# A two-layer transformer with a product-key expert layer: expert panels prepared on another queue, gate columns one batch ahead, another order of the expert blocks

## The chip, the cores and the metric

One core of one Trainium2 chip runs the kernel. The metric is the device time of one execution in microseconds; of several runs the median is shown. TensorE is called PE, VectorE DVE, ScalarE ACT, GpSimd POOL and SyncE SP, as in the profile.

## What is computed

The input is x, 512 tokens of 1024 floats. Block 1 has two layers, each an attention mixer (stick-breaking and sparse attention in the first, forgetting attention in the second) and a feed-forward layer with a convolution and a gate. Block 2 is a neighbourhood attention with a gated MLP, and then the layer that most of the change is about: PEER, a feed-forward layer of 128 x 128 experts, each one row u and one row v. A token's query picks 16 experts in each of 8 heads:

```
idx, g = top-16 of product keys (two tables of 128), softmax over the 16
y[t] = sum over the 128 picked (head, k):  g * gelu(h[t] . u[idx]) * v[idx]
x = rmsnorm(x + gate * y)
```

All of it is float32. The weights of the 16384 experts are read as 128 panels `peer_u[i]` and 128 panels `peer_v[i]`, each 128 x 1024 (512 KB).

## The kernel before, in words

**Matmuls in three parts.** A float32 product is made of three matmuls of a reduced type: high x high, high x low, low x high (`mm3`, L175 to L181). A weight panel is loaded by SP into `raw` (L166), its high part `wh` is cast by ACT (L168) and its low part `wl` is the difference, made by DVE (L173). `raw`, `wh` and `wl` have three buffers each. A scheduler orders the instructions of each engine when the program is built; every engine then runs its list in order. SP's list holds the loads, and an issue that waits holds up all behind it.

**Panels made ahead.** While the feed-forward layer of layer 1 (`ffn(1)`, L866, 1036 to 1290 us of the trace) runs, `pre_steps` (L134) splits the first NPRE = 48 panels of `peer_u` for PEER: a load into one of three quarters of the tile `pre` (L139, L142), the cast on ACT into the fourth quarter (L145), the difference on DVE over the loaded data (L146), and a store of it to the DRAM tensor `Ul` (L148). Loads and stores are SP's. `ffn` takes one step after each panel `wi` and after each token tile. Later `prep_now` loads `wl` from `Ul` for panels below NPRE (L171) in place of the difference L173.

**PEER's stages.** 384 of the 512 tokens go through all panels as dense matmuls, with a gate matrix that is zero for the experts not picked; the last 128 tokens have their rows fetched one by one, by POOL's indirect loads ("gathers", 512 KB each, L1354, into the tiles `ring` and `gat`): 128 of u, used on DVE as dot products with `h2t` (L1362), and 128 of v, added into `acc` on DVE (L1373). A gather starts after a one-column POOL copy (L1353) that waits for a recent tile, so that gathers follow the program; its use comes GD = 6 gathers later.

- Top-k: `peer_topk` picks the experts while `u_block` (L1330) runs u panels beside it: matmuls, a gelu on ACT (L1338), and a store of the activations to `Ad`.
- Gates (2045 to 2296 us): `peer_g` (L1628) builds the gate matrix of 16 tokens at a time, 24 batches. Two tables `oB` and `Ag` of ones and zeros on DVE (L1633, L1636), a product on DVE for 8 tokens (L1639) and 8 scalings on ACT for the others (L1643), 32 matmuls on PE (L1648), four copies on ACT into `gst` (L1649) and a store to `Gd`. Beside each batch one or two u panels run, and two gathers are called for with their uses.
- v stage (2330 us to the end): 128 blocks, one v panel each. SPILL = 72 blocks have their activations in `Ad` and load them as `A` (L1445); the other 56 ("fresh") run their u panel now. A block multiplies the activations by `G` (eight blocks' gates, L1440, three buffers), splits the result into `wth` and `wtl` (L1463, L1465), and runs 18 matmuls over the v panel into six PSUM banks. The first 5 blocks are fresh; then spilled and fresh ones alternate until the fresh ones are used up, and 21 spilled blocks come last. After each block 214/118 gathers are called for. The last LASTV = 3 blocks run bank by bank, with the final norm (`finish`, L1476) behind.

Of the kernel before, what the change touches and what calls it, by code (L numbers as in the profile page):

```python
# [15 lines left out]
AF = mybir.ActivationFunctionType  # L16
ALU = mybir.AluOpType
# [4 lines left out]
P = 128  # L22
# [11 lines left out]
NKEY = 128  # L34
TB = 16
TD = T - P
NTB = TD // TB
GI = 8
GD = 6
SPILL = 72  # L40
NPRE = 48
FIRST = 5
LASTV = 3
EG = 10
GSTOP = 3
# [5 lines left out]
class Builder:  # L51
# [82 lines left out]
    def pre_steps(self):  # L134

        nc = self.nc
        b = self.big.tile([P, 4, D], F32, name="pre", tag="big")
        hi, u = b[:, 3].bitcast(F32R), self.I["peer_u"]
        nc.sync.dma_start(b[:, 0], u[0])  # L139
        for i in range(NPRE + 1):  # L140
            if i + 1 < NPRE:
                nc.sync.dma_start(b[:, (i + 1) % 3], u[i + 1])  # L142
            if i < NPRE:
                r = b[:, i % 3]
                nc.scalar.copy(hi, r)  # L145
                nc.vector.tensor_sub(r.bitcast(F32R), r, hi)  # L146
            if i:
                nc.sync.dma_start(self.Ul[i - 1], b[:, (i - 1) % 3])  # L148
            yield

    def look_ahead(self):
# [714 lines left out]
    def ffn(self, l, filler=None, ctx=None, pre=None):  # L866
        nc, tc, I = self.nc, self.tc, self.I
        h = self.norm_t()
        pre = pre or iter(())
        wi, wo = I[f"ffn_wi{l}"], I[f"ffn_wo{l}"]  # L870
        with ExitStack() as cx:
            ap = cx.enter_context(tc.tile_pool(name="ffp", bufs=1))
            gp = cx.enter_context(tc.tile_pool(name="ffg", bufs=2))
            if ctx:
                next(ctx)
            cv = ap.tile([P, NF, 4], F32, name="cv")
            nc.sync.dma_start(cv, I[f"ffn_cv{l}"])
            for f0 in range(NF % GF - GF, NF, GF):
                fs = list(range(max(f0, 0), f0 + GF))
                gh = gp.tile([P, GF, T], F32R, name="gh")  # L880
                gl = gp.tile([P, GF, T], F32R, name="gl")
                for q, f in enumerate(fs):
                    if f == 0:
                        first = self.panels_h([wi[0], wi[1]], h)
                    pa = first.pop(0) if first else self.panel_a(wi[2 * f], h)
                    next(pre, None)
                    pb = first.pop(0) if first else self.panel_a(wi[2 * f + 1], h)
                    next(pre, None)
                    tm = gp.tile([P, T], F32, name="tm")
                    nc.scalar.activation(tm, pa, AF.Identity, scale=cv[:, f, 2:3], bias=cv[:, f, 3:4])  # L890
                    nc.vector.scalar_tensor_tensor(tm[:, 1:], pa[:, :T - 1], cv[:, f, 1:2], tm[:, 1:],
                                                   op0=ALU.mult, op1=ALU.add)
                    nc.vector.scalar_tensor_tensor(tm[:, 2:], pa[:, :T - 2], cv[:, f, 0:1], tm[:, 2:],
                                                   op0=ALU.mult, op1=ALU.add)
                    silu = nc.scalar.activation(tm, tm, AF.Silu)
                    nc.vector.tensor_mul(tm, tm, pb)
                    nc.scalar.copy(gh[:, q], tm)
                    nc.vector.tensor_sub(gl[:, q], tm, gh[:, q])
                    if filler:
                        filler()  # L900
                    if ctx and f == 3:
                        next(ctx)
                if f0 + GF == NF:
                    self.sqrt_table(silu)
                w = []
                for f in fs:
                    raw = self.wp.tile([P, D], F32, name="raw", tag="raw", bufs=3)
                    nc.sync.dma_start(raw, wo[f])
                    wh = gp.tile([P, D], F32R, name="woh", bufs=5)
                    nc.scalar.copy(wh, raw)  # L910
                    wl = gp.tile([P, D], F32R, name="wol", bufs=5)
                    nc.vector.tensor_sub(wl, raw, wh)
                    w.append((wh, wl))
                for t in range(NT):
                    for c in range(2):
                        ps = self.st_() if c else self.tt_()
                        for q in range(len(fs)):
                            self.mm3(ps, (gh[:, q, t * P:(t + 1) * P], gl[:, q, t * P:(t + 1) * P]),
                                     (w[q][0][:, c * T:(c + 1) * T], w[q][1][:, c * T:(c + 1) * T]),
                                     q == 0, q == len(fs) - 1)  # L920
                        xs = self.x[:, t, c * T:(c + 1) * T]
                        nc.vector.tensor_add(xs, xs, ps)
                    next(pre, None)
                    if f0 + GF == NF and t == 1 and self.nx:
                        self.norm_half()
# [372 lines left out]
    def peer(self):  # L1298
        nc, tc, I = self.nc, self.tc, self.I
        self.look = 0  # L1300
        with ExitStack() as c0:
# [3 lines left out]
            Gd = dp.tile([NTB, P, NKEY, TB], F32, name="Gd")  # L1305
            ap = ec(tc.tile_pool(name="pep", bufs=1))
            wk = ec(tc.tile_pool(name="pew", bufs=2))
# [21 lines left out]
            last = [None]  # L1329
# [61 lines left out]
                    yield  # L1391

            gs = gathers()
            gk = ExitStack()
            ep = gk.enter_context(tc.tile_pool(name="pee", bufs=2))
            with ExitStack() as ck:
                kk = ck.enter_context(tc.tile_pool(name="pek", bufs=2))
                steps = self.peer_topk(kk, h, idx, it128, eid, g3, ep)
                for kind in steps:
                    if kind is None:  # L1400
                        break
                    if kind:
                        u_block()
            gp = gk.enter_context(tc.tile_pool(name="peg", bufs=2))
            for tb in range(NTB):
                behind[0] = self.peer_g(gp, idx, it128, tb, Gd)
                if tb == 4:
                    next(steps, None)
                u_block()
                if tb % 2:  # L1410
                    u_block()
                for _ in range(2 if tb < NTB - GSTOP else 0):
                    next(gs, None)
# [9 lines left out]
            rest = list(range(spilled, NKEY))  # L1423
            back = list(range(spilled))
            order, rest = rest[:FIRST], rest[FIRST:]
            while rest or back:
                if back:
                    order.append(back.pop(0))
                if rest and len(rest) * (len(back) + 1) >= len(back) * 1:
                    order.append(rest.pop(0))  # L1430
            early = {i: u_block(True, n < 4) for n, i in enumerate(order[:FIRST])}
            st = {}
            ng = 2 * P - 2 * (NTB - GSTOP)
            NM = NKEY - EG

            def g_load(n):
                k = order[n] // GI
# [59 lines left out]
            for n, i in enumerate(order[:NKEY - LASTV]):  # L1497
                w = nxt
                nxt = v_pre(n + 1)
                v = self.prep(I["peer_v"][i])  # L1500
                for t in range(NT - 1):
                    for c in range(2):
                        v_mm(n, t, c, w, v)
                for _ in range(min(ng, ng * (n + 1) // NM) - min(ng, ng * n // NM)):
                    next(gs, None)
            for _ in gs:
                pass
# [117 lines left out]
        yield None  # L1625
        flush()

    def peer_g(self, wk, idx, it, tb, Gd):  # L1628

        nc = self.nc  # L1630
        ia, ib, g = idx
        oB = wk.tile([P, TB, NKEY], F32, name="oB")
        nc.vector.tensor_tensor(oB, it.unsqueeze(1).broadcast_to([P, TB, NKEY]),  # L1633
                                ib[:, tb * TB:(tb + 1) * TB].unsqueeze(2).broadcast_to([P, TB, NKEY]), op=ALU.is_equal)
        Ag = wk.tile([P, TB, NKEY], F32, name="Ag")
        last = nc.vector.tensor_tensor(Ag, it.unsqueeze(1).broadcast_to([P, TB, NKEY]),  # L1636
                                       ia[:, tb * TB:(tb + 1) * TB].unsqueeze(2).broadcast_to([P, TB, NKEY]), op=ALU.is_equal)
        n = TB // 2
        last = nc.vector.tensor_tensor(Ag[:, 0:n], Ag[:, 0:n],  # L1639
                                       g[:, tb * TB:tb * TB + n].unsqueeze(2).broadcast_to([P, n, NKEY]), op=ALU.mult)  # L1640
        for t in range(n, TB):
            tt = tb * TB + t
            nc.scalar.activation(Ag[:, t], Ag[:, t], AF.Copy, scale=g[:, tt:tt + 1])  # L1643
        st = wk.tile([P, NKEY, TB], F32, name="gst")
        for q in range(TB // 4):
            ps = self.tt_() if q % 2 else self.st_()
# [1 line left out]
                nc.tensor.matmul(ps[:, t * P:(t + 1) * P], oB[:, q * 4 + t], Ag[:, q * 4 + t], start=True, stop=True)  # L1648
            nc.scalar.copy(st[:, :, q * 4:q * 4 + 4].rearrange("p i t -> p t i"), ps.rearrange("p (t i) -> p t i", t=4))  # L1649
        nc.sync.dma_start(Gd[tb], st)  # L1650
        return last


    def run(self, stages):
# [179 lines left out]
```

## Time and profile before

| | us |
|---|---|
| median of 3 runs | 3111.69 |
| lowest and highest run | 3098.77, 3112.72 |
| profiled execution, its own time | 3097.51 |
| its span in the trace | 3095.7 |
| PE busy | 3011.1 (97%) |
| feed-forward layer 1 in the trace | 1036 to 1290 |
| PEER's gates | 2045 to 2296 |
| v stage | 2330 to 3096 |

Busy time of one engine says little by itself here, since PE is busy 97% of the span; what is read are the stretches in which it is not, and what it waits for in them. The trace is of one execution, whose time lies 14.2 us under the median of the runs. A wait is written "engine line <- what ended it". A window's row shows, for its stretch, each engine's busy time, the clock that PE was granted (1.00 is the full one) and the share of time in which the DMA engines were moving data.

### The profile page before, as it was taken

Reading aid. Unit: us, or ns where it says so; the run is one execution under the profiler, and the core shown is the slowest. Engines: PE = TensorE matmul, PEld = TensorE weight load, DVE = VectorE, ACT = ScalarE, POOL = GpSimd, SP = SyncE. Lnnn points to the kernel's source line nnn. Section 1 sums busy time; section 2 is a strip of 40 time slices with the busy share of each in tenths; the row PEclk is TensorE's granted clock in tenths of the full one; section 3 lists DMA queues with packets and bytes.
Section 4 is the critical chain, followed back from the end, with each engine's and each line's share of the span. In section 5 each row is a group of like instructions: output and inputs, shape, how many; then the busy total and the mean of one; then the engine's idle time right before and its main releaser. Section 6 shows DMA issues by size and latency. Waiting matters only on the chain. (4 is left out here: it accounts for less than half of the span.)

```text
span 3095.7 us, 42567 instructions
## 1 busy us (share of the span) xinstructions
PE 3011.1 (97%) x15688; PEld 2548.0 (82%) x15688; DVE 2152.5 (70%) x3986; ACT 1419.3 (46%) x2398; POOL 579.4 (19%) x609
## 2 busy tenths in 40 slices
PE   8999999999999999999999999999899999999988
PEld 6877787788777777788888889999898888888876
DVE  3378798645577766546853689848857777787878
ACT  4466532224455554335663344467663333333333
POOL 2400000000000000000000100013335565554552
PEclk9999999999999999999999999999999999999999
DMA  4210266524211689534332326899789899999986
GB/s 133 69 42 22 90 190 221 186 82 138 92 55 50 210 302 310 198 105 138 108 102 89 116 77 209 285 341 330 265 298 322 303 342 320 336 322 339 317 315 217
DMA packets 224073, 617.88 MB, mean 200 GB/s; under 512 B 20684, under 2 KB 89452, under 8 KB 220396
## 3 DMA queue, kind: packets, MB, share of 16 engines
q1 hardware_dynamic: 186424, 479.87, 46.7%
q0 software_dynamic: 36864, 134.23, 12.0%
q8 instruction: 124, 2.03, 0.3%
q10 hardware_dynamic: 576, 1.05, 0.1%
q14 instruction: 85, 0.70, 0.1%
HBM read 547.34 MB, written 67.73 MB: 199 GB/s over the span
## 5 line engine op out<-in xcount | busy, mean ns | idle before, releaser
L168 ACT CAST wh<-raw 128x1024 fp32r<-128x1024 f32 (+1 forms) x478 | 501.0, 1048 | 974.5 <-PE mm L180 348.6
L173 DVE TENSOR_TENSOR wl<-raw,wh 128x1024 fp32r<-128x1024 f32 (+1 forms) x412 | 504.6, 1228 | 388.0 <-ACT wh L168 384.6
L179 PE MATMUL mm<-bh,wh 128*128 128x384 f32 (+2 forms) x1656 | 599.1, 362 | 4.7 <-ACT wh L168 4.5
L181 PE MATMUL mm<-bh,wl 128*128 128x384 f32 (+2 forms) x1656 | 594.9, 359 | 2.4 <-DVE wl L173 1.5
L180 PE MATMUL mm<-bl,wh 128*128 128x384 f32 (+2 forms) x1656 | 595.1, 359 | 0.0
L179 PEld LDWEIGHTS mm<-bh,wh 128*128 128x128 f32 x1656 | 311.7, 188 | 37.6 <-ACT wh L168 6.5
L181 PEld LDWEIGHTS mm<-bh,wl 128*128 128x128 f32 x1656 | 311.6, 188 | 34.5 <-DVE wl L173 3.3
L180 PEld LDWEIGHTS mm<-bl,wh 128*128 128x128 f32 x1656 | 311.8, 188 | 30.7 <-issue 0.3
L180 PE MATMUL acc<-wl,wth 128*128 128x512 f32 x768 | 303.3, 395 | 11.9 <-DVE wl L173 11.7
L181 PE MATMUL acc<-wh,wtl 128*128 128x512 f32 x768 | 302.7, 394 | 0.0
L179 PE MATMUL acc<-wh,wth 128*128 128x512 f32 x768 | 292.4, 391 | 4.1 <-ACT wth L1463 2.3
L179 PE MATMUL mx<-bh,wh 128*128 128x512 f32 (+3 forms) x616 | 228.1, 370 | 0.0
L180 PE MATMUL mx<-bl,wh 128*128 128x512 f32 (+3 forms) x616 | 225.2, 366 | 0.0
L181 PE MATMUL mx<-bh,wl 128*128 128x512 f32 (+3 forms) x616 | 225.0, 365 | 0.0
L1137 POOL MEMSET bt<- 128x256 f32 x2 | 0.6, 316 | 1043.0 <-PE sc L181 1043.0
L180 PEld LDWEIGHTS acc<-wl,wth 128*128 128x128 f32 x768 | 145.6, 190 | 44.4 <-DVE wl L173 15.1
L179 PEld LDWEIGHTS acc<-wh,wth 128*128 128x128 f32 x768 | 145.0, 189 | 34.3 <-ACT wth L1463 3.1
L181 PEld LDWEIGHTS acc<-wh,wtl 128*128 128x128 f32 x768 | 145.7, 190 | 31.1 <-DVE wtl L1465 0.9
L181 PEld LDWEIGHTS mx<-bh,wl 128*128 128x128 f32 (+1 forms) x616 | 115.2, 187 | 16.1 <-DVE wl L173 0.3
L179 PEld LDWEIGHTS mx<-bh,wh 128*128 128x128 f32 (+1 forms) x616 | 115.2, 187 | 15.6 <-issue 0.7
L180 PEld LDWEIGHTS mx<-bl,wh 128*128 128x128 f32 (+1 forms) x616 | 115.3, 187 | 15.1 <-issue 0.5
L1463 ACT CAST wth<-w 128x384 fp32r<-128x384 f32 x128 | 65.6, 513 | 92.2 <-DVE w L1459 81.6
(593 smaller groups left out, 6147.7 us busy)
## 6 DMA issues: line engine op xcount, KB each, us to landing
raw<-in_peer_u SPq DMA_DIRECT2D x128, 512.0 KB, 5.1
raw<-in_peer_v SPq DMA_DIRECT2D x128, 512.0 KB, 6.8
raw<-in_ffn_wi SPq DMA_DIRECT2D x88, 512.0 KB, 4.4
araw<-in_ada_w SPq DMA_DIRECT2D x48, 512.0 KB, 4.1
pre<-in_peer_u SPq DMA_DIRECT2D x48, 512.0 KB, 5.3
Ul<-pre SPq DMA_DIRECT2D x48, 512.0 KB, 5.2
wl<-Ul SPq DMA_DIRECT2D x48, 512.0 KB, 4.7
Gd<-gst SPq DMA_DIRECT2D x24, 1024.0 KB, 7.3
```

Of the source, the lines that this page charges most:

```text
L168: nc.scalar.copy(wh, raw)
L173: (nc.gpsimd if on_pool else nc.vector).tensor_sub(wl, raw, wh)
L179: nc.tensor.matmul(out, ah, bh, start=first, stop=False)
L180: nc.tensor.matmul(out, ah, bl, start=False, stop=False)
L181: nc.tensor.matmul(out, al, bh, start=False, stop=last)
L1137: nc.gpsimd.memset(bt[:, 4], 0.0)
L1463: nc.scalar.copy(wh, w)
```

## The change

1. NPRE goes from 48 to 32, and the loads and stores of `pre_steps` are issued by POOL. `ffn` gets the steps only from its fourth column group on.
2. `peer_pair` makes `oB` and `Ag` for the next batch right after the matmuls of this one. Six gathers are issued in top-k.
3. The v stage's order spreads the 51 fresh blocks evenly among the 72 spilled ones.
4. Gathers are called for in proportion to a weight of 1 for a spilled block and 2 for a fresh one.

```diff
-NPRE = 48
+NPRE = 32
...
-                nc.sync.dma_start(b[:, (i + 1) % 3], u[i + 1])
+                nc.gpsimd.dma_start(b[:, (i + 1) % 3], u[i + 1])
...
-                nc.sync.dma_start(self.Ul[i - 1], b[:, (i - 1) % 3])
+                nc.gpsimd.dma_start(self.Ul[i - 1], b[:, (i - 1) % 3])
...
-        pre = pre or iter(())
+        steps, pre = pre or iter(()), iter(())
...
-                    if ctx and f == 3:
-                        next(ctx)
+                    if f == 3:
+                        if ctx:
+                            next(ctx)
+                        pre = steps
...
+                    if n > 28 and n % 4 == 0:
+                        next(gs)
+                        ng -= 1
...
+            behind[0], pair = self.peer_pair(gp, idx, it128, 0)
             for tb in range(NTB):
-                behind[0] = self.peer_g(gp, idx, it128, tb, Gd)
+                self.peer_g(gp, pair, tb, Gd)
+                if tb + 1 < NTB:
+                    behind[0], pair = self.peer_pair(gp, idx, it128, tb + 1)
...
-            while rest or back:
-                if back:
-                    order.append(back.pop(0))
-                if rest and len(rest) * (len(back) + 1) >= len(back) * 1:
-                    order.append(rest.pop(0))
+            nr, nb = len(rest), len(back)
+            for n in range(nr + nb):
+                order.append((rest if (n + 1) * nr // (nr + nb) > n * nr // (nr + nb) else back).pop(0))
...
-            NM = NKEY - EG
+
+            wt = [1 if i < spilled else 2 for i in order[:NKEY - EG]]
+            due = [ng * sum(wt[:n]) // sum(wt) for n in range(len(wt) + 1)]
...
-                for _ in range(min(ng, ng * (n + 1) // NM) - min(ng, ng * n // NM)):
+                for _ in range(due[n + 1] - due[n] if n < len(wt) else 0):
                     next(gs, None)
```

`peer_pair` holds the DVE and ACT part of the old `peer_g`, unchanged; its lines are now L1643 (both tables) and L1646 (the product). The lists of instructions move so:

**SP in the feed-forward layer 1.** Before, where the steps begin (L139, L142 and L148 are the steps', L166 and L908 the layer's panels):

```order
107 L877 DMA cv<-in_ffn_cv 128x88
108 L139 DMA pre<-in_peer_u 128x1024
109 L142 DMA pre<-in_peer_u 128x1024 x2
110 L148 DMA Ul<-pre 128x1024
111 L166 DMA raw<-in_ffn_wi 128x1024
112 L142 DMA pre<-in_peer_u 128x1024
113 L148 DMA Ul<-pre 128x1024 x2
114 L142 DMA pre<-in_peer_u 128x1024
115 L166 DMA raw<-in_ffn_wi 128x1024
```

Now, the same place on SP:

```order
107 L877 DMA cv<-in_ffn_cv 128x88
108 L166 DMA raw<-in_ffn_wi 128x1024 x2
109 L910 DMA raw<-in_ffn_wo 128x1024 x2
110 L166 DMA raw<-in_ffn_wi 128x1024 x8
```

and on POOL, which had only fills and copies there:

```order
59 L1062 COPY fold<-idn 32x32 x4
60 L139 DMA pre<-in_peer_u 128x1024
61 L142 DMA pre<-in_peer_u 128x1024 x2
62 L148 DMA Ul<-pre 128x1024
63 L142 DMA pre<-in_peer_u 128x1024
64 L148 DMA Ul<-pre 128x1024 x2
```

The steps have left SP's list and stand in POOL's in the same pattern. On ACT the first cast L145 stands at the same place of the list as before. Before, 29 casts stand among the first 23 of the layer's panel casts and 48 among 42; now all 32 stand among the first 23.

**DVE in the gate stage.** Before, at the fourth and fifth batch (L1362 is the use of a gather, row tiles `ring` and `gat`):

```order
2523 L1633 TENSOR_TENSOR oB<-it_15199,ix_15197 128x2048
2524 L1636 TENSOR_TENSOR Ag<-it_15199,ix_15196 128x2048
2525 L1639 TENSOR_TENSOR Ag<-Ag,ix_15198 128x1024
2526 L1362 ISA ring,act_15203<-ring,h2t 128x1024
2527 L1362 ISA act_15203 128x1
2528 L1362 ISA gat,act_15203<-gat,h2t 128x1024
2529 L1362 ISA act_15203 128x1
2530 L1633 TENSOR_TENSOR oB<-it_15199,ix_15197 128x2048
```

Now, from the first batch on:

```order
2503 L1643 TENSOR_TENSOR oB<-it_15135,ix_15133 128x2048
2504 L1643 TENSOR_TENSOR Ag<-it_15135,ix_15132 128x2048
2505 L1643 TENSOR_TENSOR oB<-it_15135,ix_15133 128x2048
2506 L1646 TENSOR_TENSOR Ag<-Ag,ix_15134 128x1024
2507 L1643 TENSOR_TENSOR Ag<-it_15135,ix_15132 128x2048
2508 L1646 TENSOR_TENSOR Ag<-Ag,ix_15134 128x1024
2509 L1364 ISA ring,act_15139<-ring,h2t 128x1024
2510 L1364 ISA act_15139 128x1
2511 L1364 ISA gat,act_15139<-gat,h2t 128x1024
2512 L1364 ISA act_15139 128x1
2513 L173 TENSOR_TENSOR wl<-raw,wh 128x1024 x7
2514 L1643 TENSOR_TENSOR oB<-it_15135,ix_15133 128x2048
```

Uses (now L1364) begin behind the second batch's tables, not behind the fourth's: 42 of them fall among the 24 batches, where 36 did. Some differences `wl` have moved in between.

**SP at the end of the v stage.** Before, the last blocks are spilled ones:

```order
687 L1445 DMA A<-Ad 128x384
688 L166 DMA raw<-in_peer_v 128x1024
689 L1445 DMA A<-Ad 128x384
690 L166 DMA raw<-in_peer_v 128x1024
```

Now they are mixed, and the last block is a fresh one:

```order
519 L1453 DMA A<-Ad 128x384 x2
520 L166 DMA raw<-in_peer_u 128x1024
521 L166 DMA raw<-in_peer_v 128x1024 x3
522 L1453 DMA A<-Ad 128x384
523 L166 DMA raw<-in_peer_u 128x1024
524 L166 DMA raw<-in_peer_v 128x1024 x2
```

The `G` loads, which from the third on stood 7 to 11 v panels ahead of their first use in the list of SP before, stand 0 to 3 ahead of it for five of the sixteen now, since a new one takes the buffer of one that is needed longer.

## Rows read from the trace of the kernel before

**Rows 1.** The page: busy us of each engine, share of span, instructions.

```profile
PE 3011.1 (97%) x15688; PEld 2548.0 (82%) x15688; DVE 2152.5 (70%) x3986; ACT 1419.3 (46%) x2398; POOL 579.4 (19%) x609
```

**Rows 2.** Windows by stage: busy us of each engine, then clock, DMA share and GB/s.

```profile
1036.00:1182.00 146.00, 136.05 (x613) 109.32 (x612) 103.05 (x125) 80.13 (x106) 0.00 (x0) 0.99 0.87 293
1182.00:1290.00 108.00, 103.90 (x449) 83.19 (x448) 69.27 (x76) 47.29 (x55) 0.00 (x0) 1.00 0.84 286
...
2045.00:2296.00 251.00, 235.95 (x1594) 234.48 (x1593) 195.32 (x165) 186.13 (x347) 92.10 (x84) 0.97 0.86 307
...
2330.00:2985.00 655.00, 652.74 (x3143) 574.00 (x3142) 513.48 (x653) 240.31 (x320) 359.80 (x382) 1.00 0.93 325
2985.00:3020.00 35.00, 24.08 (x95) 18.92 (x94) 24.16 (x28) 7.62 (x10) 21.26 (x17) 0.85 0.84 293
3020.00:3096.00 76.00, 64.08 (x270) 50.81 (x268) 63.63 (x91) 26.71 (x47) 21.54 (x21) 0.94 0.60 216
```

**Rows 3.** Waits of PE, 1036 to 1290 us: total us, times, longest us.

```profile
PE mm L179 <- ACT wh L168: 4.5, 3, 3.0
```

**Rows 4.** Waits of SP's queue, 1036 to 1290 us.

```profile
SPq L148 <- DVE pre L146: 72.4, 29, 7.9
SPq L142 <- DMA Ul<-pre: 48.3, 34, 3.7
```

**Rows 5.** The tile `pre`, 1036 to 1290 us: each line's ns (min/median/max), first and last start.

```profile
L145 ACT CAST pre<-pre x48: 1029/1050/1057, 1040.9 to 1279.6; 128x1024 fp32r<-128x1024 f32 x48
L146 DVE TENSOR_TENSOR pre<-pre x48: 1214/1225/1227, 1041.9 to 1280.7; 128x1024 fp32r<-128x1024 f32 x48
```

**Rows 6.** DMA issues, 1036 to 1290 us: count, KB each, median us to landing.

```profile
pre<-in_peer_u SPq DMA_DIRECT2D x48, 512.0 KB, 5.3
Ul<-pre SPq DMA_DIRECT2D x48, 512.0 KB, 5.2
```

**Rows 7.** Waits of DVE, 2045 to 2296 us.

```profile
DVE oB L1633 <- PE tp L1648: 55.0, 5, 49.0
DVE gat L1362 <- DMA gat<-in_peer_ut,eid: 18.1, 10, 3.4
DVE ring L1362 <- DMA ring<-in_peer_ut,eid: 12.8, 5, 3.6
```

**Rows 8.** Waits of PE, 2045 to 2296 us.

```profile
PE sc L1648 <- ACT gst L1649: 13.7, 4, 5.1
```

**Rows 9.** Groups by line, 2045 to 2296 us: count, busy us, mean ns, idle time before.

```profile
L1633 DVE TENSOR_TENSOR oB<-it,ix 128x2048 f32<-128x2048 f32 x22 | 50.3, 2288 | 55.0 <-PE tp L1648 55.0
...
L173 DVE TENSOR_TENSOR wl<-raw,wh 128x1024 fp32r<-128x1024 f32 x25 | 30.5, 1221 | 9.3 <-ACT wh L168 9.3
```

**Rows 10.** DMA issues, 2045 to 2296 us.

```profile
raw<-in_peer_u SPq DMA_DIRECT2D x35, 512.0 KB, 6.6
...
gat<-in_peer_ut,eid POOLq DMA_INDIRECT x21, 9.9
```

**Rows 11.** DMA issues, 2330 to 2985 us.

```profile
raw<-in_peer_v SPq DMA_DIRECT2D x106, 512.0 KB, 6.9
raw<-in_peer_u SPq DMA_DIRECT2D x51, 512.0 KB, 5.1
G<-Gd SPq DMA_DIRECT2D x13, 1536.0 KB, 15.0
...
ring<-in_peer_vt,eid POOLq DMA_INDIRECT x55, 7.7
```

**Rows 12.** The tile `ring`, 2330 to 2985 us: POOL's issues, min/median/max ns.

```profile
L1354 POOL DMA_INDIRECT ring<-in_peer_vt,eid x55: 962/1333/1944, 2618.2 to 2983.8; - x55
```

**Rows 13.** Waits of PE, 2985 to 3096 us.

```profile
PE acc L180 <- DVE wl L173: 11.7, 3, 10.9
```

**Rows 14.** The chain of waits, 2980 to 3015 us: start us, us, what.

```profile
2991.24 12.03 DMA raw<-in_peer_v
...
3005.33 1.22 DVE wl L173
```

More of the change, by code (lines that the diff above doesn't have):

```diff
@@ L138, in pre_steps @@
         hi, u = b[:, 3].bitcast(F32R), self.I["peer_u"]
-        nc.sync.dma_start(b[:, 0], u[0])
+        nc.gpsimd.dma_start(b[:, 0], u[0])
         for i in range(NPRE + 1):
             if i + 1 < NPRE:
-                nc.sync.dma_start(b[:, (i + 1) % 3], u[i + 1])
+                nc.gpsimd.dma_start(b[:, (i + 1) % 3], u[i + 1])
             if i < NPRE:
@@ L1393, in peer @@
             gs = gathers()
+            ng = 2 * P - 2 * (NTB - GSTOP)
             gk = ExitStack()
@@ L1398, in peer @@
                 steps = self.peer_topk(kk, h, idx, it128, eid, g3, ep)
-                for kind in steps:
+                for n, kind in enumerate(steps):
                     if kind is None:
@@ L1425, in peer @@
             order, rest = rest[:FIRST], rest[FIRST:]
-            while rest or back:
-                if back:
-                    order.append(back.pop(0))
-                if rest and len(rest) * (len(back) + 1) >= len(back) * 1:
-                    order.append(rest.pop(0))
+            nr, nb = len(rest), len(back)
+            for n in range(nr + nb):
+                order.append((rest if (n + 1) * nr // (nr + nb) > n * nr // (nr + nb) else back).pop(0))
             early = {i: u_block(True, n < 4) for n, i in enumerate(order[:FIRST])}
             st = {}
-            ng = 2 * P - 2 * (NTB - GSTOP)
-            NM = NKEY - EG
+            wt = [1 if i < spilled else 2 for i in order[:NKEY - EG]]
+            due = [ng * sum(wt[:n]) // sum(wt) for n in range(len(wt) + 1)]
             def g_load(n):
@@ L1626, in peer_topk, with peer_pair, peer_g @@
         flush()
-    def peer_g(self, wk, idx, it, tb, Gd):
+    def peer_pair(self, wk, idx, it, tb):
         nc = self.nc
-        ia, ib, g = idx
+        ia, ib, g = [q[:, tb * TB:(tb + 1) * TB] for q in idx]
         oB = wk.tile([P, TB, NKEY], F32, name="oB")
-        nc.vector.tensor_tensor(oB, it.unsqueeze(1).broadcast_to([P, TB, NKEY]),
-                                ib[:, tb * TB:(tb + 1) * TB].unsqueeze(2).broadcast_to([P, TB, NKEY]), op=ALU.is_equal)
         Ag = wk.tile([P, TB, NKEY], F32, name="Ag")
-        last = nc.vector.tensor_tensor(Ag, it.unsqueeze(1).broadcast_to([P, TB, NKEY]),
-                                       ia[:, tb * TB:(tb + 1) * TB].unsqueeze(2).broadcast_to([P, TB, NKEY]), op=ALU.is_equal)
+        for o, ix in ((oB, ib), (Ag, ia)):
+            nc.vector.tensor_tensor(o, it.unsqueeze(1).broadcast_to([P, TB, NKEY]),
+                                    ix.unsqueeze(2).broadcast_to([P, TB, NKEY]), op=ALU.is_equal)
         n = TB // 2
-        last = nc.vector.tensor_tensor(Ag[:, 0:n], Ag[:, 0:n],
-                                       g[:, tb * TB:tb * TB + n].unsqueeze(2).broadcast_to([P, n, NKEY]), op=ALU.mult)
+        last = nc.vector.tensor_tensor(Ag[:, 0:n], Ag[:, 0:n], g[:, 0:n].unsqueeze(2).broadcast_to([P, n, NKEY]), op=ALU.mult)
         for t in range(n, TB):
-            tt = tb * TB + t
-            nc.scalar.activation(Ag[:, t], Ag[:, t], AF.Copy, scale=g[:, tt:tt + 1])
+            nc.scalar.activation(Ag[:, t], Ag[:, t], AF.Copy, scale=g[:, t:t + 1])
+        return last, (oB, Ag)
+    def peer_g(self, wk, pair, tb, Gd):
+        nc = self.nc
+        oB, Ag = pair
         st = wk.tile([P, NKEY, TB], F32, name="gst")
@@ L1650, in peer_g @@
         nc.sync.dma_start(Gd[tb], st)
-        return last
     def run(self, stages):
```

## The prediction, made before the change was run

> **What bounds the kernel now.** I read the page first: PE is busy 97% of the span [rows 1], so a change of order can only win the other 3%, and stretches at a low clock. The windows by stage [rows 2] say where those are. The reader should take span less PE busy, stage by stage. The feed-forward layer 1 (1036 to 1290 us) leaves 10.0 and 4.1 us, the gate stage (2045 to 2296) 15.1, the v stage up to 2985 only 2.3, and its end (2985 to 3096) 10.9 and 11.9. The clock adds to this: PE has two levels, 2.4 and 1.2 GHz, and a mean of 0.97 over the 251 us of the gate stage means some 15 us at the lower one, of which 7 are lost; the 0.85 of 2985 to 3020 costs some 5 of 35. All the change's places are among these, so I then read for each one who ends PE's waits.
>
> In the feed-forward layer the longest waits are for ACT's cast `wh` [rows 3], since ACT's list is in order and the steps' casts stand in it. The steps' own pace is 48 casts from 1040.9 to 1279.6 [rows 5], (1279.6 - 1040.9)/47 = 5.08 us. In SP's queue the steps' store waits 72.4 us for DVE and their next load 48.3 us for a store [rows 4]; layer panels stand behind both. In the gate stage DVE waits 18.1 and 12.8 us for gathers to land [rows 7] (the 49 us before the first table lie at the stage's edge), and PE 13.7 us for `gst` [rows 8]: a use that waits on DVE holds up the next batch's tables behind it, hence ACT's scalings and copies, hence PE. At the end, the largest single wait is 10.9 us of PE [rows 13], and the chain names the cause: a v panel's load that took 12.03 us [rows 14] where the stage's median is 6.9 [rows 11].
>
> **The change part by part.**
>
> **Gate stage.** Tables come one batch earlier than the matmuls that need them, so a late gather no longer reaches PE at once, and each use comes one batch, some 9 us, later behind its gather than before; a gather lands in 9.9 us there [rows 10]. The waits of 18.1 and 12.8 us should all but go. What replaces them: DVE's own work. A batch is 2.29 for each of two tables and 1.22 for the product (that of a difference over 128x1024 [rows 9]), 5.80 in all, 24 x 5.80 = 139 us. Uses, also 1.22, go from 36 to 42: 51 us. Differences go from 25 [rows 9] to about 37, as 16 fewer panels find theirs made and the order puts most of these 16 here: 45 us. Together 235 us, before 213, beside a PE that needs 251 - 15.1 - 7 = 229. Some 18 of DVE's 235 lie before the first batch's matmuls, so DVE fits, at 95%, with little slack: I leave a third of the 22 us lost now. Gain 14, bounds 0 (DVE becomes the bound) and 18.
>
> **v stage.** The blocks' own matmuls stay; what moves is when the DMAs are wanted. A matmul over 512 columns takes (136.05 + 103.90)/(613 + 449) = 0.226 us [rows 2], so the 18 of a spilled block 4.07. In that time the 21 spilled blocks at the end ask for a panel (0.52 MB), `A` and an eighth of `G` (0.2 each) and 214/118 = 1.81 gathers (0.95 MB): 1.87 MB in 4.07 us, 459 GB/s, and no stage in the windows moves over 325 [rows 2]. That is the 12.03 us landing. Spread, with one gather unit for a spilled block and two for a fresh one, the demand is even, about 335 to 343 GB/s over the whole stage where it now runs at 325 with DMA busy 0.93 [rows 2]. So the end's waits turn into a demand of 0.98 all along. Of the 22.8 us that PE is idle after 2985 about 10 stay (the final norm behind the last matmul); I count 12 gained with the clock's share. Against this: a `G` load lands in 15.0 us [rows 11], and five of them are now issued 0 to 3 blocks ahead of use, 0 to 19 us at a mean of 6.2 a block; PE's own lead covers most, and I count 4 us for them and the doubled gathers of the first five blocks. Net gain 8, bounds -7 (each of the five 3 us late) and 17.
>
> **Feed-forward layer 1.** Sixteen steps go (16 casts of 1.05 and 16 differences of 1.22 [rows 5], 32 DMAs), and SP is freed of the 72.4 and 48.3 us. But the other 32 are not spread: by the order they all stand among 23 panel casts, where 29 stood before. So the pace of a step decides. Three quarters rotate: load 5.3, cast 1.05, difference 1.22, store 5.2 are 12.8 us [rows 5, 6], and 3 x 5.08 = 15.2, so some 2.5 are waits for ACT, DVE and SP's list. On POOL the trace shows no plain load. From below: landing as on SP, and half of the waits gone with SP's list, s = 4.7. From above: both land like v gathers, 7.7 [rows 11], with 4.8 for the rest and the waits, s = (15.4 + 4.8)/3 = 6.7. I take 5.25: an issue on POOL itself takes 1.33 us [rows 12], against about a third of that on SP, 2 us more for the two, less the 1.5 of SP's list, (15.2 + 2.0 - 1.5)/3. The 23 panels need about 127.6 us of PE (23 x 24 matmuls of 0.226, and transposes), and ACT leads PE by about two panels, 11 us. Hence PE's loss is 31 s - 138.6: 24 us at 5.25, where 15.4 are lost now (14.1 idle, and clock). Behind the 23rd panel no step is left and the loss ends. Net loss 9; at 4.7 a gain of 8, at 6.7 a loss of 54. The 16 loads `wl` from `Ul` that go later (5.2 MB less) and their 16 differences lie in top-k and gates, beside PE, and are counted above. If that cover were gone, 16 x 1.22 = 20 us.
>
> The Trainium skill, page "DMA: Bandwidth & Descriptors", section "Issuing engines are not separate DMA queues", says that initiating on several engines only saves the time that a sequencer takes to initiate. By it this part would be worth nothing beyond the casts removed; SP's waits in [rows 4] are waits in order, not initiating time, so the trace shows more to save than the page grants.
>
> **Sum.** -14 - 8 + 9 = -13 us: from the profiled execution's 3097.5 to 3084.5. That execution lies 14.2 us under the median of the runs, so against the median 3111.7 the forecast is 3098.7, and the runs of one build alone spread from 3098.8 to 3112.7.
>
> **The rivals.**
>
> *Steps paced by POOL* (slower). If POOL's loads and stores take what gathers take, s = 6.7, the first part costs 54 us and the sum is +32: 3143.7. It undoes the whole change from 31 s - 138.6 - 15.4 = 22, s = 5.7. For it: gathers land later than raw panels in the same stage, 9.9 against 6.6 [rows 10], and POOL's issue is stretched to 1.94 [rows 12]. Against it: gathers come in pairs and fetch single rows, these are whole panels. Chance 0.15.
> The Trainium skill, page "SBUF — State Buffer", section "SBUF: two separate sides", warns of this: DMAs issued from GpSimd wait for their descriptors while DVE holds a shared port. The trace agrees as far as POOL's issue goes, 0.96 at the least and 1.94 at the most [rows 12].
>
> *SP freed pays in full.* s = 4.7 or less; layer panels come early, and the first part gains 8: -14 - 8 - 8 = -30, 3081.7. For it: the 121 us of SP's waits [rows 4] that go. Against: the denser casts. Chance 0.28.
>
> *The v stage keeps its time.* At 0.98 DMA demand and with late `G` loads new waits of 8 us take the place of the end's: -14 + 9 = -5, 3106.7. For it: 0.93 busy already, `G` at 15.0 [rows 11]; against: the end asks for 459 now. Chance 0.20.
>
> *DVE becomes the gate stage's bound.* 235 us of work on a 229 us PE and nothing gained: -8 + 9 = +1, 3112.7. Chance 0.07.
>
> *It does not do what it says* holds for "later": the first cast stands at the same place of ACT's list as before. That is in the sum, not apart.
>
> **How the numbers follow.** The forecast has 0.30. About 0.5%, 15.6 us, is what a measurement of this kernel can tell from no change. The forecast of -13 lies just inside it, so I give it 0.43 for faster; SP freed nearly all of its 0.28; the others little: faster 0.42. Slower by over 15.6 needs s over 6.2, most of the POOL case, and a late `G` beside a bad pace: 0.15. The same: 0.43. The range runs from the SP case with the v stage's best, and the runs' own spread, 3068, to 3126, which takes in the DVE and v cases and the near part of the POOL case and leaves out its far end.
>
> **What would show it.** In the changed profile: the span of the cast L145 over its 31 gaps gives s (5.25; over 5.7 the POOL case, under 4.9 the SP case); PE idle in the feed-forward layer 24 to 28 us; no DVE wait for `ring` or `gat` over 3 us in the gate stage, and PE idle there under 8; GB/s in the v stage 335 or more, and no wait of PE over 5 us near its end. I am wrong if the v stage shows waits of DVE for `G` over 10 us in sum, or the gate stage DVE busy over 97%.

## The result and the profile after

The changed kernel takes 3145.54 us (median of 4 runs, 3140.66 to 3152.66) against 3105.57 of the kernel before in the same measurements: ratio 1.013, 95% interval 1.0094 to 1.0166, so 1.3% slower. The forecast was 13 us faster; the range ended at 3126.

I cut both traces at the same three instructions: the last column group of the feed-forward layer 1 that goes through `mm` (its start of L893), the first and the last gate matmul (`oB`, `Ag`). The 1036 to 1290 us given ahead for this layer are only its part with steps beside it; the layer goes on past the cut. The differences add up to the span's 48.4 us:

| stage, us | before | after | difference | forecast |
|---|---|---|---|---|
| to the end of feed-forward layer 1 | 1380.5 | 1396.6 | +16.1 | +9 |
| from there to the first gate matmul | 664.6 | 664.9 | +0.3 | 0 |
| gates | 250.0 | 227.4 | -22.6 | -14 |
| from the last gate matmul to the end | 800.6 | 855.2 | +54.6 | -8 |

The medians lie 40.0 us apart and not 48.4: the traced execution of the kernel before (3097.51) is 8.1 us under its median, that of the changed kernel (3146.12) 0.6 over. In which stage those 8 us lie, one trace of the kernel before does not show. Of the 61.4 us between forecast and trace the v stage makes 62.6; the other stages nearly cancel.

The windows of the changed kernel (busy us of PE, PEld, DVE, ACT, POOL, then clock, DMA share, GB/s), where [rows 2] has those of before:

```profile
1036.00:1182.00 146.00, 129.26 (x551) 102.00 (x550) 94.54 (x115) 72.05 (x96) 30.12 (x57) 0.94 0.82 283
1182.00:1290.00 108.00, 102.25 (x424) 81.76 (x423) 55.29 (x65) 37.53 (x45) 4.02 (x8) 0.95 0.44 144
2062.00:2289.00 227.00, 227.00 (x1585) 227.00 (x1584) 209.78 (x183) 186.20 (x346) 114.27 (x84) 1.00 0.89 315
2330.00:2985.00 655.00, 611.36 (x2810) 524.87 (x2809) 472.11 (x603) 217.01 (x291) 302.08 (x349) 0.96 0.88 304
2985.00:3020.00 35.00, 35.00 (x171) 30.86 (x170) 29.48 (x31) 11.96 (x16) 22.69 (x23) 1.00 0.93 323
3020.00:3144.00 124.00, 107.28 (x500) 92.09 (x498) 85.21 (x113) 45.42 (x71) 27.39 (x28) 0.95 0.56 192
```

In the gates PE is busy 227.00 of 227 us at full clock. The v stage, which had been busy 652.74 of 655, is idle for 43.6 us at a clock of 0.96, while DMA is *less* busy (0.88 against 0.93). A stage that waits while its DMA engines are less used than before is hardly short of bandwidth, so I looked for an order that holds loads back. The waits of PE over the whole trace of the changed kernel:

```profile
PE acc L179 <- ACT wth L1471: 40.2, 14, 6.9
...
PE tp L179 <- ACT woh L912: 7.3, 7, 2.3
PE tp L180 <- DVE wol L914: 6.8, 8, 1.3
PE mm L179 <- ACT wh L168: 6.4, 4, 2.4
```

and over that of the kernel before:

```profile
PE acc L179 <- ACT wth L1463: 2.3, 2, 1.9
```

Here is the longest of the 14, from the timeline of the changed kernel (start us, us, engine, line, operation; in brackets the idle time before it and what ended it), cut to SP and to the rows that lead to PE:

```profile
2770.45 0.43 SPq L1448 DMA_DIRECT2D G<-Gd  x1
...
2775.53 7.11 SPq L1453 DMA_DIRECT2D A<-Ad  x1
...
2782.74 0.91 SPq L166 DMA_DIRECT2D raw<-in_peer_v  x1
...
2791.86 1.04 ACT L168 CAST wh<-raw 128x1024 fp32r<-128x1024 f32 x1 [10.69 <-DMA raw<-in_peer_v]
2792.82 0.48 ACT L1340 ACTIVATE act<-mm 128x384 f32<-128x384 f32 x1
2792.94 1.23 DVE L173 TENSOR_TENSOR wl<-raw,wh 128x1024 fp32r<-128x1024 f32 x1 [9.32 <-ACT wh L168]
2794.09 0.55 DVE L1467 TENSOR_TENSOR w<-G,act 128x384 f32<-128x384 f32 x1
...
2795.23 0.79 PE L179 MATMUL acc<-wh,wth 128*128 128x512 f32 x1 [6.89 <-ACT wth L1471]
```

Read from below: PE waits for the split product `wth`; DVE's product `w` stands behind the difference `wl` of a later v panel, and ACT's gelu `act` behind that panel's cast. The panel landed late, since its load was issued at 2782.74, behind an `A` load that held SP 7.11 us, behind a `G` load. The gelu and `w` need nothing of that panel; they wait for it because ACT and DVE run their lists in order. The same piece in the kernel before has the same lists, with a panel that is on time:

```profile
2700.69 1.05 ACT L168 CAST wh<-raw 128x1024 fp32r<-128x1024 f32 x1 [2.95 <-PE mm L180]
...
2701.64 0.48 ACT L1338 ACTIVATE act<-mm 128x384 f32<-128x384 f32 x1
2701.78 1.23 DVE L173 TENSOR_TENSOR wl<-raw,wh 128x1024 fp32r<-128x1024 f32 x1 [2.35 <-ACT wh L168]
2702.92 0.55 DVE L1459 TENSOR_TENSOR w<-G,act 128x384 f32<-128x384 f32 x1
...
2703.50 1.04 ACT L1463 CAST wth<-w 128x384 fp32r<-128x384 f32 x2 [1.38 <-DVE w L1459]
```

From the end of the u panel's matmuls (2700.6) to a finished `wth` this chain takes 3.5 to 4 us, and PE has one block's 18 matmuls, 4.07 us, to cover it. So the lead was almost nothing before as well; any lateness of a panel there goes straight to PE. Over the whole stage, from the end of the cast to the first matmul that takes `wth`, the lead of the 51 fresh blocks that follow a spilled one is 0.73 us (median) in the kernel before; that of the spilled blocks behind a fresh one is 8.5.

### The profile page after: what moved, and what is told of

Same layout as the page of the kernel before. It is cut to its first block, busy times and chain, and to the rows that moved or that the text cites. A ratio compares the mean times of both kernels' runs of the same rounds, so it can differ in the third digit from the quotient of the medians.

```text
span 3144.1 us, 42405 instructions
## 1 busy us (share of the span) xinstructions
PE 3031.6 (96%) x15680; PEld 2557.2 (81%) x15688; DVE 2150.6 (68%) x3986; ACT 1404.5 (45%) x2384; POOL 605.6 (19%) x673
## 4 chain that ended last, share of the span: by engine, by line
PE 66%; DMA 11%; DVE 11%; ACT 4%; issue 3%; SPq 1%; POOL 0%; DVEq 0%; ACTq 0%; POOLq 0%
PE mm L181 9%; PE mm L179 9%; PE mm L180 9%; DMA raw<-in_peer_u 5%; PE mx L181 4%; PE mx L180 4%; PE mx L179 4%; PE acc L179 3%; PE acc L181 3%; PE acc L180 3%; DVE wl L173 2%; PE tp L482 2%; DMA raw<-in_ffn_wo 2%; DMA pre<-in_peer_u 1%; DMA raw<-in_peer_v 1%
## 5 line engine op out<-in xcount | busy, mean ns | idle before, releaser
L173 DVE TENSOR_TENSOR wl<-raw,wh 128x1024 fp32r<-128x1024 f32 (+1 forms) x428 | 523.5, 1228 | 507.8 <-ACT wh L168 473.7
L179 PE MATMUL acc<-wh,wth 128*128 128x512 f32 x768 | 308.2, 401 | 42.6 <-ACT wth L1471 40.2
L139 POOL DMA_DIRECT2D pre<-in_peer_u x1 | 0.8, 753 | 659.8 <-DVE bl L271 659.8
L1471 ACT CAST wth<-w 128x384 fp32r<-128x384 f32 x128 | 64.6, 513 | 99.4 <-DVE w L1467 98.0
```

Source lines behind the costliest of these rows:

```text
L139: nc.gpsimd.dma_start(b[:, 0], u[0])
L173: (nc.gpsimd if on_pool else nc.vector).tensor_sub(wl, raw, wh)
L179: nc.tensor.matmul(out, ah, bh, start=first, stop=False)
L1471: nc.scalar.copy(wh, w)
```

## The experiments

Every run was timed beside the kernel before, and the ratio is to that; the stages are those of the table above, from one profiled execution each (those of e3 and e8 took 6.4 and 10.1 us more than their medians). Where nothing in a stage differs they scatter: e1, e8, e9 and e10 have the same v stage at 788.1 to 793.0 us, and the changed kernel's feed-forward layer ends at 1392.2 to 1400.7 in the nine traces that have it.

| run | FF layer end | gates | v stage | time | ratio, 95% |
|---|---|---|---|---|---|
| e1 | 1393.7 | 227.4 | 788.6 | 3080.44 | 0.9899 to 0.9955 |
| e2 | 1398.1 | 227.5 | 835.6 | 3132.28 | 1.0064 to 1.0132 |
| e3 | 1400.7 | 227.4 | 825.2 | 3114.04 | 1.0002 to 1.0041 |
| e4 | 1379.2 | 227.5 | 792.8 | 3068.76 | 0.9859 to 0.9914 |
| e5 | 1395.1 | 227.4 | 849.9 | 3142.24 | 1.0087 to 1.0150 |
| e6 | 1399.8 | 227.5 | 813.2 | 3105.98 | 0.9983 to 1.0020 |
| e7 | 1384.0 | 227.5 | 790.0 | 3066.69 | 0.9838 to 0.9898 |
| e8 | 1384.3 | 227.4 | 793.0 | 3061.98 | 0.9819 to 0.9880 |
| e9 | 1379.1 | 227.4 | 788.1 | 3062.18 | 0.9802 to 0.9901 |
| e10 | 1395.4 | 227.5 | 788.7 | 3078.68 | 0.9878 to 0.9944 |
| e11 | 1400.1 | 227.5 | 814.5 | 3106.36 | 0.9972 to 1.0022 |
| e12 | 1392.2 | 227.5 | 784.2 | 3072.83 | 0.9874 to 0.9923 |
| e13 | 1380.0 | 227.4 | 787.7 | 3061.35 | 0.9834 to 0.9885 |
| e14 | 1394.3 | 227.4 | 804.0 | 3098.20 | 0.9957 to 0.9996 |
| e15 | 1382.3 | 227.4 | 782.7 | 3059.72 | 0.9812 to 0.9874 |

**Which part costs (e1 to e4).** e1, against the changed kernel, puts the old loop over the order of blocks back (the diff's "-" lines of part 3); e2 sets the weights equal:

```diff
-            wt = [1 if i < spilled else 2 for i in order[:NKEY - EG]]
+            wt = [1 for i in order[:NKEY - EG]]
```

> The changed kernel with the v stage's old order of blocks (51 pairs of a spilled and a fresh block, then 21 spilled ones); gathers keep the new weights. In the changed kernel the v stage, from the last gate matmul to the end, takes 855 us, before 801. Theory 1 (the spread order itself makes panels late, by what it puts ahead of their loads in SP's list): back to 790 to 805, the whole kernel about 3090. Theory 2 (the weight of two gathers for a fresh block makes bursts that delay the panels): 840 or more, since the bursts stay.

> The changed kernel with gathers called for evenly, as before; the new order of blocks stays. Theory 1 (order): v stage stays at 845 to 860 us. Theory 2 (bursts of gathers): v stage back to 790 to 810, waits of PE for wth mostly gone.

e1 gives 66.6 us of v stage back: the order is the cause. But e2 gives 19.6 back too, where theory 1 said none: bursts of gathers matter, though only with the new order (with the old one, e7 against e4, the weights win 3 us or nothing, 790.0 against 792.8).

e3 moves G's loads to another queue:

```diff
-                    nc.sync.dma_start(st[k], Gd[...
+                    nc.scalar.dma_start(st[k], Gd[...
```

> The changed kernel with the 16 loads of G issued by ACT's queue and not by SP's. The eight waits of PE over 1.5 us (37 us in sum) each come 11 to 33 us behind a G load on SP, whose next issue then takes 4 to 12 us. Theory 3 (the issue behind a G load blocks SP, and panels behind it come late): most of the 37 us go, v stage 815 to 825. If G only matters as traffic, or if A loads waiting for w are the cause, v stage stays at 845 or more.

30.0 us came back, the edge of theory 3's range. The Trainium skill, page "DMA: Bandwidth & Descriptors", section "Queues, rings and completion order", says that a DMA engine takes turns between the queue rows of the issuers; moved to ACT's row, `G` no longer stands ahead of the panels in theirs, and e3 agrees with that.

e4 is the kernel before with `peer_pair` and the early gathers alone.

> The kernel before with the gate part of the change alone (tables one batch ahead, six gathers in top-k). From the two traces the gate stage went from 250.0 to 227.4 us; if that is this part's own, and nothing of it comes back in the v stage: 15 to 25 us faster than before, about 3080. If what it wins is given back by the v stage, within 5 us of before.

It is 1.1% faster: 22.5 us in the gates, and 7.8 in the v stage, which is left with 208 gather units and not 214; the 7.8 are little more than the scatter.

**What makes the new order late (e5, e6, e11, e12, e14).** e5 changes the range of `a_load` (`n + 4, n + 5` to `n + 2, n + 3`); e6 does that with e2's and e3's edits; e11 has e2's and e3's edits, with `A` loads issued by `nc.gpsimd`.

> The changed kernel with the loads of A issued two blocks ahead of use and not four. Theory A (in the new order four buffers of A are reused so soon that a load's issue waits in SP's list for the product w just before, 98 us in sum, and panels' loads stand behind it): those waits of SP go down to under 30 us, and the v stage from 855 to 830 to 840 us. If only the G loads and the bursts of gathers count, v stage stays within 5 us of 855.

> The changed kernel, new order of blocks kept, with all three: G loads on ACT's queue, A loads two blocks ahead, gathers called for evenly. Alone, G on ACT gave 30 us and even pace 20 us back of the 66 us that the new order costs against the old one (855.2 against 788.6). If the order costs by these three things: v stage 785 to 800. If something else in the order costs: 805 or more.

> The changed kernel, new order of blocks, even gathers, with A loads on POOL's queue and G loads on ACT's, so that in the v stage SP's list holds nothing but panels. Theory SP (what stands ahead of the panels in SP's list is all that the new order costs): v stage 785 to 800 us. If DVE's list (a product w behind the difference of a panel that lands late) is the rest: 803 to 815, with waits of PE for wth as with A two ahead (813.2, 12 waits).

e5 did not test what it was meant to: SP's waits of `A` for `w` stayed (94.1 us, in the same stretch of the changed kernel 92.6), as the scheduler kept 64 of the 72 loads at their places among SP's panels. e11 tests it: with no `A` in SP's list the v stage is 814.5, with them (e6) 813.2, so the `A` loads' place in that list shows no cost (what they cost in POOL's, no run separates). And with SP's list holding nothing but panels 22 to 26 us of the cost stay, with 11 waits of PE for `wth`.

That an issue is held behind a `G` load is not new. In the kernel before SP is held 3.6 to 9.1 us behind 11 of the 16, as here:

```profile
2628.85 0.38 SPq L1440 DMA_DIRECT2D G<-Gd  x1
2629.27 7.79 SPq L1445 DMA_DIRECT2D A<-Ad  x1
```

What is new is the panel that stands there. In SP's list of the kernel before, and of e1, the first panel behind each `G` load from the second on is a v panel; in the changed kernel it is a u panel behind 10 of the 15, and a fresh block's product needs its u panel. ACT's waits for u panels to land, 2330 to 2985 us, in the kernel before, the changed one and e14 (the run below):

```profile
ACT wh L168 <- DMA raw<-in_peer_u: 5.6, 4, 1.5
```

```profile
ACT wh L168 <- DMA raw<-in_peer_u: 99.4, 21, 9.4
```

```profile
ACT wh L168 <- DMA raw<-in_peer_u: 107.4, 24, 11.1
```

No run changes this place alone; that it is why the order costs is read from the lists.

e12 is e11 with the products made two blocks ahead; e14 is the same edit alone on the changed kernel:

```diff
-            nxt = v_pre(0)
+            q2 = [v_pre(0), v_pre(1)]
...
-                w = nxt
-                nxt = v_pre(n + 1)
+                w = q2.pop(0)
+                q2.append(v_pre(n + 2))
...
```

The edit also calls for each `G` and `A` load one block earlier.

> As the run with A and G off SP's list and even pace (new order of blocks, v stage 814.5 us), with the product w, its split, and a fresh block's u panel made two blocks ahead of the block's matmuls and not one. Theory DVE (the rest of the new order's cost is that w stands in DVE's list behind the difference of a u panel that lands late, just before PE needs w): the 11 waits of PE for wth, 16.2 us, go to under 4 us, and the v stage to 785 to 798. If panels as such come too late in the new order, the waits move to wh and wl, and the v stage stays at 808 or more.

> The changed kernel with only the products, their splits and the fresh blocks' u panels made two blocks ahead; A and G stay in SP's list and the gathers keep their weights. With G and A off SP's list and even pace the same edit took the v stage from 814.5 to 784.2 us. Theory lead (the short lead of w is the common cause, and G loads and bursts only cost because w has no lead over them): v stage 785 to 800, from 855. Theory sum (they are separate costs): the edit gives some 30 us, v stage 820 to 830.

e12 fell by 30.3 us, to the old order's level or a little below (784.2 against 788.1 to 793.0), and its waits for `wth` are gone; its row of the v stage:

```profile
2330.00:2985.00 655.00, 651.50 (x3116) 569.57 (x3115) 524.94 (x664) 235.54 (x322) 410.96 (x455) 1.00 0.96 335
```

That is DMA at 0.96 and 335 GB/s, the even demand that the new order was to give, now really moved. e14 gives 51.2 of the 66.6 us back with `G` still in SP's list and the bursts still there. That this is the lead and not the earlier calls shows in e14's trace: SP is still held 4.7 to 10.4 us behind 15 of the `G` loads and u panels are as late as in the changed kernel (107.4 us against 99.4), but the lead of a fresh block behind a spilled one is 6.1 us (median). What is left, in the waits of PE of e14 from 2320 us on, is mostly panels that are late themselves:

```profile
PE acc L180 <- DVE wl L173: 7.2, 6, 3.3
PE mm L179 <- ACT wh L168: 6.5, 3, 5.1
PE acc L179 <- ACT wth L1471: 3.3, 1, 3.3
```

So neither of e14's theories is exact (804.0, between 800 and 820, nearer to the first): late panels cost most where a product has no lead. The lead gives 51.2 of the 66.6 us back, `G`, `A` and the pace together (e11) 40.7. The 30, the 20 and the 51 us are not parts of a sum.

**Why the feed-forward layer got longer (e7 to e10).** e7 is e4 with the weights; e8 is e7 with `NPRE = 32`; e10 is e8 with POOL's loads and stores as in the change; e9 adds an order to e10's casts:

```diff
-                nc.scalar.copy(hi, r)
+                with self.tc.issue_after(self.pre_after.ins):
+                    nc.scalar.copy(hi, r)
...
-                    nc.scalar.copy(gh[:, q], tm)
+                    self.pre_after = nc.scalar.copy(gh[:, q], tm)
```

> The kernel before with the gate part and the weights for gathers, but the old order of blocks and the old feed-forward layer. By the stages of the runs so far: front of the run with gates alone (to 2272.0 us) and the v stage of the run with the old order and the weights (788.6): span 3060.6, time about 3064, 4 us under gates alone. If the weights do nothing for the old order: as gates alone, 3069.

> As the run with gates and weights, but 32 panels made ahead and not 48, on SP's queue. By the order, the 32 casts then stand among 29 panel casts as in the kernel before, not among 23. Theory density (the feed-forward layer loses 14 to 20 us in the changed kernel since 32 steps of 5.15 us stand among 23 panels): here the layer ends at most 2 us later than before (1380.5), more likely some us earlier. Theory panels (fewer panels made ahead lose time elsewhere): top-k or gates get longer than 665 and 227 us.

> As the run with 32 panels made ahead on SP (same gates, weights and order of blocks), but loads and stores on POOL's queue, and each cast ordered behind the last gated column group, so that the 32 casts stand among 30 panel casts and not among 22 or 23. Theory density (the pace of a step is about 5.2 us on either queue, and the loss comes from 32 steps among 23 panels): the feed-forward layer ends by 1386 us, as on SP (1384.3). Theory POOL (POOL's queue itself costs): 1393 or later, as in the changed kernel (1396.6).

> The same without that ordering: by the order, the 32 casts on POOL's queue stand among 22 panel casts. Theory density: the layer ends at 1396 to 1403 us, 12 to 20 us later than with the casts spread, and the kernel at 3075 to 3085. If the place of the casts does not matter: by 1388.

The casts' first and last start, in the changed kernel, e8 (SP), e9 (POOL, spread) and e10 (POOL, dense), one line of the tile `pre` of each kernel:

```profile
L145 ACT CAST pre<-pre x32: 1032/1048/1057, 1039.8 to 1199.4; 128x1024 fp32r<-128x1024 f32 x32
```

```profile
L145 ACT CAST pre<-pre x32: 1029/1049/1058, 1038.8 to 1200.4; 128x1024 fp32r<-128x1024 f32 x32
```

```profile
L150 ACT CAST pre<-pre x32: 1032/1048/1056, 1038.6 to 1209.9; 128x1024 fp32r<-128x1024 f32 x32
```

```profile
L145 ACT CAST pre<-pre x32: 1029/1050/1057, 1038.9 to 1192.6; 128x1024 fp32r<-128x1024 f32 x32
```

Divided by 31 gaps a step takes 5.15, 5.21, 5.53 and 4.96 us. The queue makes no difference that shows to the pace; the kernel with the quickest steps ends the layer 16 us later than the one with the slowest (1395.4 against 1379.1). These two differ only in where the 32 casts stand, among 22 panel casts or among 30. Theory density holds. Taking 16 panels less ahead costs nothing that shows: top-k 665.6 in e8, 664.6 before.

**Together (e13, e15).** e13 is e9 with the products two ahead, e15 is e12 with e9's spread steps.

> The best kernel so far (gates, weights, old order of blocks, 32 panels made ahead on POOL, spread among the layer's casts; v stage 788.1) with the products two blocks ahead. If the lead of w also limits the old order: its waits for wth there (4 us) go, v stage 780 to 786. If not: 786 to 792.

> The run with products two ahead, A and G off SP's list, even pace and the new order, with the steps of the panels made ahead spread among the layer's casts (on POOL): front to 2272 us as in the spread run, v stage 784: span 3056, time 3058, 4 us under the best so far, within the error of one comparison. If the parts disturb each other: 3062 or more.

On the old order the longer lead does nothing (787.7 against 788.1): ACT waits for its u panels only 7.6 us in e9. e15 is the fastest median here, 1.6% under the kernel before, but e7, e8, e9 and e13 lie within its interval; which of the five is best is open, and so is whether the new order, with all of it mended, is worth anything (3059.72 against 3061.35 in e13). What is not open is that the gate part alone (e4, 1.1%) brings most of it, and that spread steps keep the feed-forward layer where it was (1379.1 to 1382.3 against 1380.5).

## Why the prediction was wrong

**v stage: the step that failed** is "PE's own lead covers most, and I count 4 us". I had read how far ahead of their first use the `G` loads are issued, but not how long before PE's need `w` is made. The kernel before's timeline shows a chain of 3.5 to 4 us under a cover of 4.07, and a median lead of 0.73 us; with a lead like that a late panel costs its whole lateness. The loads that were priced were the wrong ones too. The bound of 7 us ("each of the five 3 us late") looked at `G` loads that come late for their product, and DVE has no wait for `G` in the changed kernel's v stage. What counts is the panel behind a `G` load: the five longest waits for `wth`, 4.9 to 6.9 us, come 18 to 25 us behind one each, and four of these five loads stand 5 to 13 v panels ahead of their first use. Against the 4 us of the term stands a v stage that is 54.6 us longer. The other half, that the end's own waits go, came true: in the last 110.7 us (before, from 2985 us on) PE is idle 10.2 us where it was 22.5, and 10 were forecast. (The row 2985 to 3020 above is earlier work in the changed kernel; a wait of 6.7 us ends at 3032, just before those last 110.7.) The weights do most of this without the new order: 13.0 us in e7, 20.2 in e4.

**"The end's waits turn into a demand of 0.98 all along"** was wrong as well: DMA went down to 0.88. With the lead alone it is 0.93 (e14), with `G` and `A` off SP's list and the even pace as well 0.96 (e12).

**Feed-forward layer: right in kind, too small.** The pace was forecast at 5.25 and is 5.15; that density decides and not the queue was the sum's reason, and e9 and e10 show it. That the pace came out so near is in part luck. An issue on POOL was priced at 1.33 us, from gathers; it took 0.53, against 0.33 on SP before. And the waits of SP's list did not go by half: in POOL's a load waits 69.0 us for a store and a store 57.7 for DVE over 32 steps; in SP's it was 48.3 and 72.4 over 48.

```profile
L142 POOL DMA_DIRECT2D pre<-in_peer_u x31: 527/532/573, 1036.4 to 1191.3; - x31
```

The formula 31 s - 138.6 gives 21 us at 5.15, 6 more than before, and 16 were measured. PE's idle time grew by 8.4 us (22.5 in the two windows, before 14.1); the rest goes with the clock, 0.94 and 0.95 where it was 0.99 and 1.00, a change that the term left out. Of two levels 0.94 over 146 us is 18 us at the lower one, 9 lost, and 0.95 over 108 us another 5; that is an estimate and more than the 7.7 us that are left, as part of the time at the lower level falls on PE's waits. The 16 loads from `Ul` that the prediction puts at 5.2 MB are 8.4 (16 of 512 KB); nothing in its sum hangs on it.

**Gates: right in kind, too small.** The waits of DVE for gathers are gone, as forecast. I left a third of the loss because of DVE's load, put at 95%; DVE is busy 209.78 of 227 us, 92%, and its waits in 2045 to 2296 us are none that reaches PE:

```profile
DVE wl L173 <- ACT wh L168: 27.0, 7, 6.5
DVE oB L1643 <- PE tp L1659: 4.0, 6, 1.4
```

DVE is now ahead and waits for PE; 22.6 us were won, all of the loss, above my bound of 18. How much of it the tables one batch ahead won, and how much the six gathers issued in top-k, no run separates.

**The rivals.** *Steps paced by POOL* named almost the measured time (3143.7) for a reason that is not there: s is 5.15, not 6.7; that it came near is luck. *SP freed* failed with the densely placed casts. *The v stage keeps its time* had the place and named `G`, but neither of its mechanisms came, a demand of 0.98 and `G` late for its use, and it had a price of 8 us for what cost 55. No rival asked what a late panel does to a product that stands behind it. Nor did either sign of being wrong appear, DVE's waits for `G` over 10 us or DVE over 97% in the gates: both watched DVE, and the cost lay in SP's and ACT's lists.

**Queues.** With DVE busy 94.5 of 146 us the steps on POOL keep SP's pace (5.15 against 5.08 us). The warning that the prediction quoted from the Trainium skill, page "SBUF — State Buffer", section "SBUF: two separate sides", does not show here (the page says it of DVE operations in a 2-port mode; no row here tells DVE's mode). For these steps the rule holds that the prediction quoted from the Trainium skill, page "DMA: Bandwidth & Descriptors", section "Issuing engines are not separate DMA queues", that issuing elsewhere saves little; for `G` the measurement decides against it, since its move gave 30 us of v stage back.

## What to carry to other kernels

Before an order is changed, measure the lead at the place where the stage meets PE: from the moment an operand is ready to the matmul that takes it. A stage that shows no waits may have a lead of under a microsecond (0.73 us here), and then any new lateness upstream is paid in full. Work that is put beside a stage ("panels made ahead") has to be spread over as much of it as its own pace needs; fewer steps packed densely into an in-order list cost more than many spread.

## What was not expected of the hardware

The next issue on SP behind a `G` load (1.5 MB, 3072 pieces of 512 bytes) took 4 to 11 us behind 15 of the 16 in the changed kernel; with `G` on ACT's queue no issue on SP took over 0.7 us in the same stretch (e3). What holds the issue is not shown. A pause costs beyond itself: behind the 6.89 us wait the granted clock was 0.50, the 1.2 GHz level, until 2801 us. The first matmul took 0.79 us where 0.39 is usual, and the next ones came every 0.43 us where 0.23 is usual. Stages with many short waits ran at a mean clock of 0.94 to 0.97.
